# Moving the SSD scan's per-head factors, exponentials and norm weights to ScalarE, spreading the sampled queries over sequences, and moving a v chunk into the scan

## The chip, the cores and the metric

The kernel runs on one core of one Trainium2 chip. The metric is the device time of one execution in microseconds (us), lower is better. The core has five engines, each with its own queue that runs in order: TensorE (PE in the profile), VectorE (DVE), ScalarE (ACT), GpSimd (POOL) and SyncE (SP), which here issues the DMAs. What one engine needs of another it waits for by semaphores.

## The reference

One layer of a decoder for a prompt of 1024 new tokens and for 8 sequences of 8 new tokens each (the sampled tokens, with states carried over). Token mixing has two parallel parts, an HGRN2 recurrence with 8 heads and a Mamba-2 SSD scan with 16 heads in 2 groups. The change lies in the scan, cut here to its core:

```python
def ssd_scan(xs, dt, a, bm, cm, s0):
    # h_t = exp(dt_t a) h_{t-1} + dt_t x_t B_t^T, y_t = h_t C_t (per head), in chunks of 128
    cum = jnp.cumsum(log_a, axis=2)
    seg = cum[:, :, :, None] - cum[:, :, None, :]
    decay = jnp.exp(jnp.where(causal, seg, -jnp.inf))
    cb = jnp.einsum('cbtgn,cbsgn->cbtsg', cm, bm)
    y_intra = jnp.einsum('cbtsg,cbtsgr,cbsgrp->cbtgrp', cb, decay, xdt)
    to_end, from_start = jnp.exp(cum[:, :, -1:] - cum), jnp.exp(cum)
    # from chunk to chunk, with the state s:
    y = jnp.einsum('btgn,bgrpn->btgrp', c_c, s) * fs_c[..., None]
    s = cd_c[..., None, None] * s + jnp.einsum('bsgn,bsgr,bsgrp->bgrpn', b_c, te_c, xdt_c)
# then: y = (y + d_skip * xs) * silu(z); y = rmsnorm(y, in 2 groups of 512) * m_norm
```

The sampled sequences go through the same scan, each from its own state `state_ssm`, and their new states are outputs. Behind the mixing come the output projection, a squared-ReLU MLP and norms.

## The kernel before

All products that need it are split into a high and a low fp32r part and summed from three matmuls (lines L203 to L205 of the profile). The program's stages follow each other: normalising and a first chunk of v, the scan stage (function `ssd`), the 8 HGRN heads (`hgrn_head`), the output projection, and the MLP.

In `ssd`, `conv_tile` computes one tile of 128 features of x, B and C (a GEMM, the convolution and its activation) and puts it into DRAM. `ssd_group(gi)` then scans one group of 8 heads over 8 chunks of 128 tokens, reading back from there. Per chunk:

- `ssd_pre` starts the loads: `em` (for each of 8 heads a 128x128 field of cumulative sums, L671), `x` (L673), `sz` (L675);
- `ssd_mid` makes `xdt` and `te` (`ssd_x`), and in `decay` turns `em` into the masked decay matrix: subtract the head's own sum and clip at 0 (L682, eight times), exponential (L684), product (L685);
- `ssd_prod` has the matmuls `pyi` (state times C, L699), `pdd` (the chunk's share of the new state, L701) and `py` (inside the chunk, L712), with the factor `fs` on `pyi` (L714);
- `ssd_end` calls `ssd_out`: gate (L748), square sum (L750), scaling (L752), transposes `pyt` on PE (L755), norm weights `ms` (L757), store.

After chunk 3 `ssd_sample` does the sampled tokens of the group. Its loop over j (four pairs of heads) loads eight states `s0` (L800; `ss` in the profile), transposes them (`pst`, L804), splits them, multiplies by the sampled C (`pis`, L808 and L809), takes each sequence's own part by predicated copies (`own_sequence`, L240), scales the states on GpSimd (L811), adds the new share (`pds` L245 and L246, L816) and stores them (L818).

Between the steps, `fill(n)` emits n tiles of other GEMMs from a list of generators (`filler`): chunks of z and of v (`z_chunk`, `v_chunk`, 9 token tiles each: 8 of 128 tokens, one of the 64 sampled). Their products lie in DRAM until later; head h of HGRN reads back its part of v (`vt`, `vs`). The order of instructions on each engine is set by a scheduler that simulates the program; what stands in a queue on the chip is then fixed. Tiles come from pools: a tag has a number of buffers (`bufs`), and a new tile of a tag waits until the oldest use has been given up. The tag `em` has 4, shared by the chunks' `em`, the sampled tokens' `ems` and `bmh`, and the states `s0`. The tags of `c2` have 2 or 3.

Of the kernel before, what the change touches and what calls it, by code (L numbers as in the profile page):

```python
# [6 lines left out]
F32 = mybir.dt.float32  # L7
F32R = mybir.dt.float32r
# [7 lines left out]
P = 128  # L16
# [3 lines left out]
NB = 8  # L20
# [37 lines left out]
class Kernel:  # L58
# [472 lines left out]
    def ssd(self):  # L531
        nc, a = self.nc, self.a
        with ExitStack() as es:
            g = self.g = es.enter_context(self.tc.tile_pool(name="sd", bufs=2, reuse_waits="tile"))
            self.dsk = g.tile([P, MH], F32, name="dsk", bufs=1)
            nc.sync.dma_start(self.dsk, a["d_skip"][0].partition_broadcast(P))
            self.cs = g.tile([P, 12, 27], F32, name="cs", bufs=1)
            self.filler = []
            for f in (10, 8, 0, 1, 2, 3):
                self.conv_tile(f)  # L540
            for j in range(2):
                for _ in self.z_chunk(j):
                    pass
            self.filler = [self.z_chunk(2), self.z_chunk(3)]
            self.ssd_group(0)
            self.fill(18)
            for f in (11, 9, 4, 5, 6, 7):
                self.conv_tile(f)
            self.filler = [self.v_chunk(1), self.v_chunk(2)]
            for q in range(3):  # L550
                pt = self.ps.tile([P, 512], F32, name=self.nm("pcs"), tag="tp", bufs=2)
                for j in range(4):
                    nc.tensor.transpose(pt[0:27, j * P:(j + 1) * P], self.cs[:, 4 * q + j, :], self.ident)
                crow = self.c2("ms", [P, 512])
                nc.scalar.copy(crow[0:27, :], pt[0:27, :])
                cols = slice(q * 512, (q + 1) * 512)
                nc.sync.dma_start(a["o_cvp"][0, 0, :, cols], crow[0:3, :])
                nc.sync.dma_start(a["o_cvs"][0, :, :, cols].rearrange("b j c -> (b j) c"), crow[3:27, :])
                self.fill(1)
            self.ssd_group(1)  # L560
            self.fill(18)
            self.filler = [self.v_chunk(3)]

# [114 lines left out]
    def decay(self, em, cbm, rows, c, h0):  # L678

        nc = self.nc  # L680
        for h in range(8):
            nc.vector.tensor_scalar(out=em[:, h, :], in0=em[:, h, :], scalar1=self.cum[0:rows, c, h0 + h:h0 + h + 1],  # L682
                                    scalar2=0.0, op0=ALU.subtract, op1=ALU.min)
        nc.scalar.activation(em, em, AF.Exp)  # L684
        nc.vector.tensor_tensor(out=em, in0=em, in1=bc(cbm, 1, 8), op=ALU.mult)  # L685
# [6 lines left out]
    def ssd_prod(self, gi, c, st):  # L692
# [20 lines left out]
        if c > 0:  # L713
            nc.vector.tensor_tensor(out=te, in0=pi.rearrange("p (h d) -> p h d", d=HD),  # L714
                                    in1=bc(self.fs[:, c, h0:h0 + 8], 2, HD), op=ALU.mult)
        nc.vector.tensor_tensor(out=x, in0=py, in1=x, op=ALU.add)
# [8 lines left out]
    def ssd_final(self, gi, st):  # L725
# [6 lines left out]
        nc.sync.dma_start(a["o_smp"][0, 0, 8 * gi:8 * gi + 8].rearrange("(j h) p n -> (h p) j n", h=2), so)  # L732

    def ssd_x(self, x, rows, c, h0):

        nc = self.nc
        xdt, te = self.c2("xdt", [P, 8, HD]), self.c2("te", [P, 8, HD])
        r = slice(0, rows)
        nc.vector.tensor_tensor(out=xdt[r], in0=x[r], in1=bc(self.dtt[r, c, h0:h0 + 8], 2, HD), op=ALU.mult)
        nc.vector.tensor_tensor(out=te[r], in0=xdt[r], in1=bc(self.te[r, c, h0:h0 + 8], 2, HD), op=ALU.mult)  # L740
        nc.vector.tensor_tensor(out=x[r], in0=x[r], in1=bc(self.dsk[r, h0:h0 + 8], 2, HD), op=ALU.mult)
        return xdt, te

    def ssd_out(self, gi, y, sz, rows, col):
# [9 lines left out]
        for j in range(4):  # L754
            nc.tensor.transpose(pt[:, j, 0:rows], y[r_, j * P:(j + 1) * P], self.ident[0:rows, 0:rows])  # L755
        ms = self.c2("ms", [P, 4, P])
        nc.vector.tensor_tensor(out=ms[:, :, 0:rows], in0=pt[:, :, 0:rows], in1=bc(self.mn[:, 4 * gi:4 * gi + 4], 2, rows),  # L757
                                op=ALU.mult)
        for c, s_ in self.places(col // P):
            nc.sync.dma_start(self.mixd[KO + 4 * gi:KO + 4 * gi + 4, :, c].rearrange("k p t -> p k t"), ms[:, :, s_])  # L760

    def ssd_sample(self, gi):
# [30 lines left out]
        ted = self.stacked(g, te.rearrange("p h d -> p (h d)"), 512, "ted")  # L793
        cts = self.beside(g, bt[:, 1, :], "cts", "bts")
        yf = self.c2("ms", [P, 4, P])
        nc.gpsimd.memset(yf, 0.0)
        for j in range(4):
# [3 lines left out]
            for hf in range(2):  # L801
# [4 lines left out]
                self.split(sth, stl, pt)  # L806
                pi = ps.tile([P, 4, P], F32, name=self.nm("pis"), tag="sm", bufs=3)
                nc.tensor.matmul(pi, cts, sth, start=True, stop=False)  # L808
                nc.tensor.matmul(pi, cts, stl, start=False, stop=True)  # L809
                self.own_sequence(yf[:, j, :], pi, 4 * hf)  # L810
            nc.gpsimd.tensor_tensor(out=s0, in0=s0, in1=bc(self.cds[:, hh // 2, :], 2, P), op=ALU.mult)  # L811
# [67 lines left out]
    def hgrn_head(self, h):  # L879
# [22 lines left out]
        nc.scalar.activation(LF, A, AF.Ln, bias=self.lb[:, h:h + 1], scale=self.oml[:, h:h + 1])  # L902
        self.fill(4)
        K = A
# [45 lines left out]

        self.fill(9)

# [635 lines left out]
```

## Time and profile before

| what | us |
|---|---|
| median of 3 runs (lowest, highest) | 1901.96 (1899.98, 1903.06) |
| the profiled execution, its span | 1905.25, 1903.5 |
| PE busy | 1816.3 (95%) |
| VectorE busy | 1345.6 (71%) |
| ScalarE busy | 865.6 (45%) |
| GpSimd busy | 447.6 (24%) |

An engine's busy time is the sum over its instructions; the share is of the span. The rows further down come from the one profiled execution, and the positions in them are microseconds from its start: group 0 of the scan runs from about 160 to 358, with convolution tiles beside it, group 1 from about 409 to 535, and head 0 of HGRN behind it.

### The profile page before, as it was taken

The numbers are of one execution on the slowest core, as the hardware profiler recorded it, in microseconds if no ns is written. First come the engines' busy times: TensorE is split into PE (matmuls) and PEld (weight loads), VectorE is DVE, ScalarE is ACT, GpSimd is POOL, SyncE is SP. The second block draws the span as 40 slices with busy tenths as digits, with TensorE's granted clock in tenths as the row PEclk, the third lists the DMA queues.
The fourth block names the chain that finished last, engine by engine and source line by source line (L and its number), as shares of the span: only waits on it lengthen the run. The fifth ranks groups of instructions, "written<-read, shape, count | busy, mean of one in ns | idle before, by whom it ended". The sixth has DMA issues, their size and how long they took to land.

```text
span 1903.5 us, 35681 instructions
## 1 busy us (share of the span) xinstructions
PE 1816.3 (95%) x13352; PEld 1742.5 (92%) x13352; DVE 1345.6 (71%) x2769; ACT 865.6 (45%) x1891; POOL 447.6 (24%) x540
## 2 busy tenths in 40 slices
PE   7989999799589999999989998999999999999998
PEld 7989988699389999999989998999999999999998
DVE  7676779777755766776684357778887757777762
ACT  8566445552234444444442355455455553323322
POOL 5110011001111333332210036223322322322320
PEclk9999999799789999999999999999999999999999
DMA  8434455445441222222167674366555586755622
GB/s 264 125 101 128 126 164 156 124 124 151 133 116 48 81 71 81 82 82 68 51 198 227 178 217 125 105 207 212 184 176 194 199 286 226 249 165 186 226 83 78
DMA packets 329495, 285.47 MB, mean 150 GB/s; under 512 B 26197, under 2 KB 268481, under 8 KB 329322
## 3 DMA queue, kind: packets, MB, share of 16 engines
q1 hardware_dynamic: 329322, 283.19, 47.6%
q8 instruction: 105, 1.72, 0.4%
q14 instruction: 68, 0.56, 0.1%
HBM read 184.61 MB, written 98.24 MB: 149 GB/s over the span
## 4 chain that ended last, share of the span: by engine, by line
PE 78%; DVE 8%; DMA 6%; ACT 4%; issue 3%; POOL 1%; SPq 1%; DVEq 0%; ACTq 0%; POOLq 0%
PE sx L1318 15%; PE mm L205 11%; PE mm L203 11%; PE mm L204 11%; PE sy L1318 7%; PE sz L1318 4%; DVE wl L199 1%; PE py L712 1%; PE mk L203 1%; PE mk L204 1%; PE mk L205 1%; DVE acc L601 1%; DVE em L682 1%; PE pf L203 1%; PE pf L205 1%
## 5 line engine op out<-in xcount | busy, mean ns | idle before, releaser
L198 ACT CAST wh<-wr 128x512 fp32r<-128x512 f32 (+3 forms) x354 | 202.4, 582 | 266.9 <-PE mm L204 90.1
L199 DVE TENSOR_TENSOR wl<-wr,wh 128x512 fp32r<-128x512 f32 (+3 forms) x354 | 233.0, 664 | 107.3 <-ACT wh L198 99.9
L203 PE MATMUL mm<-hh,wh 128*128 128x384 f32 (+1 forms) x840 | 280.0, 333 | 10.3 <-ACT raw L587 10.3
L204 PE MATMUL mm<-hl,wh 128*128 128x384 f32 (+1 forms) x840 | 281.2, 335 | 0.0
L205 PE MATMUL mm<-hh,wl 128*128 128x384 f32 (+1 forms) x840 | 280.8, 334 | 0.0
L1318 PE MATMUL sx<-th,wh 128*128 128x272 f32 x1248 | 243.7, 291 | 7.2 <-ACT u L1371 2.9
L1318 PEld LDWEIGHTS sx<-th,wh 128*128 128x128 f32 x1248 | 196.4, 189 | 12.1 <-ACT u L1371 6.0
L1318 PE MATMUL sx<-th,wl 128*128 128x272 f32 x624 | 180.3, 289 | 0.0
L203 PEld LDWEIGHTS mm<-hh,wh 128*128 128x128 f32 x840 | 159.5, 190 | 13.5 <-ACT raw L587 12.3
L205 PEld LDWEIGHTS mm<-hh,wl 128*128 128x128 f32 x840 | 159.2, 190 | 5.4 <-issue 4.4
L204 PEld LDWEIGHTS mm<-hl,wh 128*128 128x128 f32 x840 | 159.5, 190 | 2.2 <-issue 1.2
L203 PE MATMUL mm<-wh,hh 128*128 128x260 f32 (+1 forms) x512 | 149.2, 292 | 3.3 <-ACT st L373 2.2
L205 PE MATMUL mm<-wh,hl 128*128 128x260 f32 (+1 forms) x512 | 147.6, 289 | 0.1
L204 PE MATMUL mm<-wl,hh 128*128 128x260 f32 (+1 forms) x512 | 146.7, 287 | 0.0
L1318 PE MATMUL sy<-th,wh 128*128 128x272 f32 x736 | 143.1, 290 | 2.6 <-ACT th L198 2.6
L1275 POOL TENSOR_TENSOR ws<-wr 128x512 f32<-128x512 f32 (+2 forms) x36 | 45.2, 1256 | 424.8 <-DMA wr<-in_w_down_dram 195.9
L1318 PE MATMUL sx<-td,wh 128*128 128x272 f32 x672 | 131.7, 289 | 1.7 <-ACT acc L1463 1.3
L1318 PEld LDWEIGHTS sy<-th,wh 128*128 128x128 f32 x736 | 116.4, 189 | 3.8 <-ACT th L198 2.8
L1318 PEld LDWEIGHTS sx<-th,wl 128*128 128x128 f32 x624 | 118.1, 190 | 0.1
L203 PE MATMUL mm<-mh,wh 128*128 128x272 f32 x384 | 111.8, 293 | 4.4 <-DVE res L1169 4.4
L204 PE MATMUL mm<-ml,wh 128*128 128x272 f32 x384 | 111.6, 291 | 0.0
L205 PE MATMUL mm<-mh,wl 128*128 128x272 f32 x384 | 111.2, 290 | 0.0
(507 smaller groups left out, 4832.6 us busy)
## 6 DMA issues: line engine op xcount, KB each, us to landing
td<-th SPq DMA_DIRECT2D x112, 272.0 KB, 2.9
td<-td SPq DMA_DIRECT2D x112, 272.0 KB, 5.3
wr<-in_w_in_dram SPq DMA_DIRECT2D x44, 512.0 KB, 4.7
wr<-in_w_out_dram SPq DMA_DIRECT2D x32, 512.0 KB, 4.6
wr<-in_w_up_dram SPq DMA_DIRECT2D x32, 512.0 KB, 4.1
u2d<-u SPq DMA_DIRECT2D x50, 272.0 KB, 2.1
ur<-u2d SPq DMA_DIRECT2D x50, 272.0 KB, 4.9
wr<-in_w_down_dram SPq DMA_DIRECT2D x64, 192.0 KB, 2.7
```

Source lines behind the costliest of these rows:

```text
L198: nc.scalar.copy(hi, x)
L199: (engine or nc.vector).tensor_tensor(out=lo, in0=x, in1=hi.bitcast(F32), op=ALU.subtract)
L203: nc.tensor.matmul(ps, sh, mh, start=start, stop=False)
L204: nc.tensor.matmul(ps, sh, ml, start=False, stop=False)
L205: return nc.tensor.matmul(ps, sl, mh, start=False, stop=stop)
L601: nc.vector.scalar_tensor_tensor(out=acc[:, 0:w], in0=raw[:, j:j + w], scalar=self.cw[:, j, f:f + 1], in1=acc[:, 0:w], op0=ALU.mult, op1=A ...
L682: nc.vector.tensor_scalar(out=em[:, h, :], in0=em[:, h, :], scalar1=self.cum[0:rows, c, h0 + h:h0 + h + 1], scalar2=0.0, op0=ALU.subtract, ...
L712: nc.tensor.matmul(py[:, h, :], em[:, h, :], xdt[:, h, :], start=True, stop=True)
L1275: self.nc.gpsimd.tensor_tensor(out=out_, in0=x, in1=y, op=op)
L1318: nc.tensor.matmul(acc, w_[:, k, :], b_[:, cols], start=first and k == 0 and q == 0, stop=k == nk - 1 and q == 2, skip_group_check=True)
```

## The change

- `decay`: one minimum over the whole tile on VectorE, min(em, cum), and eight exponentials on ScalarE, one for each head, with the negated sum (`ncum`, new) as bias, instead of eight subtractions with clipping and one exponential.
- The factors by head, `te` in `ssd_x` and `fs` on `pyi`, become eight ScalarE copies of 64 columns with a per-partition factor each (`per_head`), and the norm weights four copies of 128 columns, instead of one VectorE product each.
- The sampled queries: GpSimd spreads C over a tile `cm` (for each sequence a 128-wide stationary matrix that is zero outside that sequence's columns), so that 16 matmuls of 128 columns per j add up in one PSUM tile; a ScalarE copy takes it out. The predicated copies go. `cm` is a tile of the tag `em`, whose buffers stay 4.
- Fillers: group 0 gets z2, z3 and v1, group 1 v2 and v3; head 0 of HGRN has none.

```diff
...
             self.dsk = g.tile([P, MH], F32, name="dsk", bufs=1)
             nc.sync.dma_start(self.dsk, a["d_skip"][0].partition_broadcast(P))
             self.cs = g.tile([P, 12, 27], F32, name="cs", bufs=1)
+            self.ncum = g.tile([P, NT, MH], F32, name="ncum", bufs=1)
+            nc.scalar.activation(self.ncum[:, 0:NC, :], self.cum[:, 0:NC, :], AF.Copy, scale=-1.0)
+            nc.scalar.activation(self.ncum[0:NS, NC, :], self.cum[0:NS, NC, :], AF.Copy, scale=-1.0)
             self.filler = []
             for f in (10, 8, 0, 1, 2, 3):
                 self.conv_tile(f)
             for j in range(2):
                 for _ in self.z_chunk(j):
                     pass
-            self.filler = [self.z_chunk(2), self.z_chunk(3)]
+            self.filler = [self.z_chunk(2), self.z_chunk(3), self.v_chunk(1)]
             self.ssd_group(0)
-            self.fill(18)
+            self.fill(27)
             for f in (11, 9, 4, 5, 6, 7):
                 self.conv_tile(f)
-            self.filler = [self.v_chunk(1), self.v_chunk(2)]
+            self.filler = [self.v_chunk(2), self.v_chunk(3)]
             for q in range(3):
                 pt = self.ps.tile([P, 512], F32, name=self.nm("pcs"), tag="tp", bufs=2)
                 for j in range(4):
...
                 self.fill(1)
             self.ssd_group(1)
             self.fill(18)
-            self.filler = [self.v_chunk(3)]
 
     C2 = {"sz": 3, "x": 3, "xdt": 3, "te": 2, "st": 3, "ms": 2}
 
...
     def decay(self, em, cbm, rows, c, h0):
 
         nc = self.nc
+        nc.vector.tensor_tensor(out=em, in0=em, in1=bc(self.cum[0:rows, c, h0:h0 + 8], 2, em.shape[2]), op=ALU.min)
         for h in range(8):
-            nc.vector.tensor_scalar(out=em[:, h, :], in0=em[:, h, :], scalar1=self.cum[0:rows, c, h0 + h:h0 + h + 1],
-                                    scalar2=0.0, op0=ALU.subtract, op1=ALU.min)
-        nc.scalar.activation(em, em, AF.Exp)
+            nc.scalar.activation(em[:, h, :], em[:, h, :], AF.Exp, bias=self.ncum[0:rows, c, h0 + h:h0 + h + 1])
         nc.vector.tensor_tensor(out=em, in0=em, in1=bc(cbm, 1, 8), op=ALU.mult)
 
     def ssd_mid(self, gi, c):
...
         for h in range(8):
             nc.tensor.matmul(py[:, h, :], em[:, h, :], xdt[:, h, :], start=True, stop=True)
         if c > 0:
-            nc.vector.tensor_tensor(out=te, in0=pi.rearrange("p (h d) -> p h d", d=HD),
-                                    in1=bc(self.fs[:, c, h0:h0 + 8], 2, HD), op=ALU.mult)
+            self.per_head(te, pi.rearrange("p (h d) -> p h d", d=HD), self.fs[:, c, h0:h0 + 8])
         nc.vector.tensor_tensor(out=x, in0=py, in1=x, op=ALU.add)
         if c > 0:
             nc.vector.tensor_tensor(out=x, in0=x, in1=te, op=ALU.add)
...
         nc.scalar.copy(so, pt)
         nc.sync.dma_start(a["o_smp"][0, 0, 8 * gi:8 * gi + 8].rearrange("(j h) p n -> (h p) j n", h=2), so)
 
+    def per_head(self, out, x, f):
+
+        for h in range(8):
+            self.nc.scalar.activation(out[:, h, :], x[:, h, :], AF.Copy, scale=f[:, h:h + 1])
+
     def ssd_x(self, x, rows, c, h0):
 
         nc = self.nc
         xdt, te = self.c2("xdt", [P, 8, HD]), self.c2("te", [P, 8, HD])
         r = slice(0, rows)
         nc.vector.tensor_tensor(out=xdt[r], in0=x[r], in1=bc(self.dtt[r, c, h0:h0 + 8], 2, HD), op=ALU.mult)
-        nc.vector.tensor_tensor(out=te[r], in0=xdt[r], in1=bc(self.te[r, c, h0:h0 + 8], 2, HD), op=ALU.mult)
+        self.per_head(te[r], xdt[r], self.te[r, c, h0:h0 + 8])
         nc.vector.tensor_tensor(out=x[r], in0=x[r], in1=bc(self.dsk[r, h0:h0 + 8], 2, HD), op=ALU.mult)
         return xdt, te
 
...
         for j in range(4):
             nc.tensor.transpose(pt[:, j, 0:rows], y[r_, j * P:(j + 1) * P], self.ident[0:rows, 0:rows])
         ms = self.c2("ms", [P, 4, P])
-        nc.vector.tensor_tensor(out=ms[:, :, 0:rows], in0=pt[:, :, 0:rows], in1=bc(self.mn[:, 4 * gi:4 * gi + 4], 2, rows),
-                                op=ALU.mult)
+        for j in range(4):
+            nc.scalar.activation(ms[:, j, 0:rows], pt[:, j, 0:rows], AF.Copy, scale=self.mn[:, 4 * gi + j:4 * gi + j + 1])
         for c, s_ in self.places(col // P):
             nc.sync.dma_start(self.mixd[KO + 4 * gi:KO + 4 * gi + 4, :, c].rearrange("k p t -> p k t"), ms[:, :, s_])
 
...
         nc.sync.dma_start(te[NS:P], te[R])
         ted = self.stacked(g, te.rearrange("p h d -> p (h d)"), 512, "ted")
         cts = self.beside(g, bt[:, 1, :], "cts", "bts")
+        cm = g.tile([P, NB, 2, NB, TS], F32R, name=self.nm("cm"), tag="em", bufs=4)
+        nc.gpsimd.memset(cm.bitcast(F32), 0.0)
+        for b in range(NB):
+            nc.gpsimd.tensor_copy(cm[:, b, :, b, :], cts.bitcast(F32).rearrange("p (a b t) -> p a b t", a=2, t=TS)[:, :, b, :])
         yf = self.c2("ms", [P, 4, P])
-        nc.gpsimd.memset(yf, 0.0)
         for j in range(4):
             hh = h0 + 2 * j
             s0 = self.em("ss0", [P, NB, P])
...
                     nc.tensor.transpose(pt[:, q, :], s0[:, 4 * hf + q, :], self.ident)
                 sth, stl = (g.tile([P, 4, P], F32R, name=self.nm("stb"), tag=t, bufs=2) for t in ("ct", "btok"))
                 self.split(sth, stl, pt)
-                pi = ps.tile([P, 4, P], F32, name=self.nm("pis"), tag="sm", bufs=3)
-                nc.tensor.matmul(pi, cts, sth, start=True, stop=False)
-                nc.tensor.matmul(pi, cts, stl, start=False, stop=True)
-                self.own_sequence(yf[:, j, :], pi, 4 * hf)
+                if hf == 0:
+                    pi = ps.tile([P, P], F32, name=self.nm("pis"), tag="sm", bufs=3)
+                for q in range(4):
+                    b = 4 * hf + q
+                    for i, st_ in enumerate((sth, stl)):
+                        nc.tensor.matmul(pi, cm[:, b].rearrange("p a s t -> p (a s t)"), st_[:, q, :],
+                                         start=b == 0 and i == 0, stop=b == NB - 1 and i == 1)
+            nc.scalar.copy(yf[:, j, :], pi)
             nc.gpsimd.tensor_tensor(out=s0, in0=s0, in1=bc(self.cds[:, hh // 2, :], 2, P), op=ALU.mult)
             for hf in range(2):
                 pd = ps.tile([P, 4, P], F32, name=self.nm("pds"), tag="sm", bufs=3)
...
         self.sigmoid_from_exp(A)
         LF = wk("lf")
         nc.scalar.activation(LF, A, AF.Ln, bias=self.lb[:, h:h + 1], scale=self.oml[:, h:h + 1])
-        self.fill(4)
         K = A
         nc.vector.tensor_scalar(out=K, in0=A, scalar1=self.noml[:, h:h + 1], scalar2=self.oml[:, h:h + 1],
                                 op0=ALU.mult, op1=ALU.add)
...
         nc.vector.tensor_tensor(out=K128, in0=KEB[:, 0:SEQ].rearrange("p (c b t) -> p c b t", b=4, t=32)[:, :, 0:2],
                                 in1=bc(fac[:, :, 9:11], 3, 32), op=ALU.mult)
 
-        self.fill(9)
 
         Dm = wk("dm")
         nc.vector.tensor_tensor(out=Dm[:, 0:SEQ].rearrange("p (b t) -> p b t", t=32),
```

SyncE issues the DMAs; these are its rows around the sampled states of group 1, before. `ss` is a state tile (its first number tells the tiles apart), L800 its load, L818 its store, and `em` the loads for chunks 5 to 7:

```order
L800 DMA ss_889_5634<-in_state_ssm_dram 128x8x128
...
L800 DMA ss_902_5706<-in_state_ssm_dram 128x8x128
...
L818 DMA o_sms_dram<-ss_889_5634 128x8x128
...
L800 DMA ss_915_5778<-in_state_ssm_dram 128x8x128
...
L818 DMA o_sms_dram<-ss_902_5706 128x8x128
L800 DMA ss_928_5850<-in_state_ssm_dram 128x8x128
...
L818 DMA o_sms_dram<-ss_915_5778 128x8x128
L671 DMA em_5950<-cumd 128x1024
L671 DMA em_6063<-cumd 128x1024
L818 DMA o_sms_dram<-ss_928_5850 128x8x128
L671 DMA em_6125<-cumd 128x1024
```

After the change, the same place (the load is now L808, the store L830, the `em` load L673):

```order
L808 DMA ss_916_6149<-in_state_ssm_dram 128x8x128
...
L830 DMA o_sms_dram<-ss_916_6149 128x8x128
...
L808 DMA ss_928_6225<-in_state_ssm_dram 128x8x128
...
L830 DMA o_sms_dram<-ss_928_6225 128x8x128
L808 DMA ss_940_6301<-in_state_ssm_dram 128x8x128
L830 DMA o_sms_dram<-ss_940_6301 128x8x128
L808 DMA ss_952_6377<-in_state_ssm_dram 128x8x128
L673 DMA em_6484<-cumd 128x1024
L830 DMA o_sms_dram<-ss_952_6377 128x8x128
L673 DMA em_6614<-cumd 128x1024
L673 DMA em_6693<-cumd 128x1024
```

A load stood ahead of the store before it; now each load stands behind it, and takes the buffer that the store gives up.

PE's rows around j=2 and j=3 of group 1's loop before. `mm` with `hh` and `wl` is a GEMM tile (here the last filler work is the 320-column block of head 0's f), `pst` the transposes of a state, `pis` and `pds` the sampled products, and `pyi` the first matmul of the scan behind the sample:

```order
L804 MATMUL pst_5796<-ident,ss_915_5778 128x128 x4
L205 MATMUL mm_6328<-hh_94,wl_6299 128x384
...
L205 MATMUL mm_6354<-hh_97,wl_6299 128x320
L808 MATMUL pis_5805<-stb_5801,cts_5629 128x512
...
L804 MATMUL pst_5852<-ident,ss_928_5850 128x128 x4
...
L804 MATMUL pst_5868<-ident,ss_928_5850 128x128 x4
...
L246 MATMUL pds_5889<-bml_5559,ted_5626 128x512
L699 MATMUL pyi_5984<-st_5468,ct_5398 128x512
```

After; the first rows here are j=1 (`ss_928`), the next ones j=2 (`ss_940`) and j=3 (`ss_952`):

```order
L812 MATMUL pst_6245<-ident,ss_928_6225 128x128 x4
L204 MATMUL mm_6952<-hl_102,wh_6896 128x320
...
L205 MATMUL mm_6952<-hh_97,wl_6897 128x320
L820 MATMUL pis_6236<-stb_6232,cm_6138 128x128
...
L812 MATMUL pst_6303<-ident,ss_940_6301 128x128 x4
L812 MATMUL pst_6321<-ident,ss_940_6301 128x128 x4
...
L812 MATMUL pst_6379<-ident,ss_952_6377 128x128 x4
L812 MATMUL pst_6397<-ident,ss_952_6377 128x128 x4
...
L700 MATMUL pyi_6518<-st_5950,ct_5880 128x512
```

The f GEMM used to end ahead of the transposes of j=3, and now it ends right behind those of j=1; j=2 and j=3 come with no other work.

PE behind group 1's last transposes, before:

```order
L729 MATMUL pst_6228<-ident,st_6191 128x128 x4
L755 MATMUL pyt_6250<-ident,x_6127 128x128 x4
L203 MATMUL mm_6405<-wh_6387,hh_90 128x260
L204 MATMUL mm_6405<-wl_6388,hh_90 128x260
L205 MATMUL mm_6405<-wh_6387,hl_98 128x260
```

And after:

```order
L729 MATMUL pst_6823<-ident,st_6776 128x128 x4
L760 MATMUL pyt_6845<-ident,x_6695 128x128 x4
L203 MATMUL mm_7025<-hh_90,wh_7017 128x384
L204 MATMUL mm_7025<-hl_98,wh_7017 128x384
L205 MATMUL mm_7025<-hh_90,wl_7018 128x384
```

Before, nine v tiles of 260 columns (the first three matmuls of 24 in the first are shown) stand ahead of head 0's Q GEMM; now the Q GEMM, with 384 columns, follows at once.

## Rows read from the trace of the kernel before

**Rows 1.** The page's first part: busy us, share, instructions of each engine.

```profile
PE 1816.3 (95%) x13352; PEld 1742.5 (92%) x13352; DVE 1345.6 (71%) x2769; ACT 865.6 (45%) x1891; POOL 447.6 (24%) x540
```

**Rows 2.** Windows: busy us and instruction counts of each engine in four stretches.

```profile
core 0: us, PE busy (x) PEld busy (x) DVE busy (x) ACT busy (x) POOL busy (x), PEclk, DMA share, GB/s
240.00:340.00 100.00, 97.30 (x611) 87.36 (x611) 84.20 (x214) 51.16 (x113) 14.48 (x23) 1.00 0.52 153
340.00:380.00 40.00, 28.06 (x150) 25.32 (x149) 29.61 (x74) 21.70 (x52) 3.25 (x8) 0.74 0.44 127
480.00:535.00 55.00, 31.08 (x133) 20.87 (x132) 45.84 (x121) 15.61 (x38) 6.40 (x16) 0.70 0.37 109
535.00:577.00 42.00, 39.81 (x283) 39.20 (x282) 17.24 (x20) 16.03 (x29) 8.48 (x13) 0.94 0.49 138
```

**Rows 3.** PE timeline, end of group 0: start, us, line, idle before and its releaser.

```profile
354.65 1.11 PE L755 MATMUL pyt<-ident,x 128*128 128x128 f32 x4 [6.74 <-ACT x L752]
```

**Rows 4.** PE timeline, end of group 1, from the last filler to the last transpose.

```profile
480.15 0.31 PE L205 MATMUL mm<-hh,wl 128*128 128x320 f32 x1
480.30 0.39 PE L808 MATMUL pis<-stb,cts 128*128 128x512 f32 x1
480.52 0.40 PE L245 MATMUL pds<-bmh,ted 128*128 128x512 f32 x1
...
481.84 0.63 PE L804 MATMUL pst<-ident,ss 128*128 128x128 f32 x4 [0.50 <-DMA ss<-in_state_ssm_dram]
...
506.77 2.56 PE L755 MATMUL pyt<-ident,x 64*128 64x64 f32 x12 [14.09 <-ACT x L752]
...
513.83 2.08 PE L701 MATMUL pdd<-te,btok 128*128 128x512 f32 x2 [4.50 <-DVE te L740]
...
534.46 1.09 PE L755 MATMUL pyt<-ident,x 128*128 128x128 f32 x4 [0.19 <-DVE ms L757]
```

**Rows 5.** Groups by line and shape, VectorE, the scan stage: busy us, mean ns.

```profile
L682 DVE TENSOR_SCALAR em<-em,cum 128x128 f32<-128x128 f32 x128 | 29.4, 300 | 6.2 <-DMA em<-cumd 5.2 <-issue 1.0
...
L685 DVE TENSOR_TENSOR em<-em,cbm 128x1024 f32<-128x1024 f32 x16 | 19.2, 1215 | 0.3 <-ACT em L684 0.3
...
L240 DVE COPY_PREDICATED ms<-seqm,pis 128x128 f32<-128x128 uint32 x64 | 18.7, 298 | 6.7 <-PE pis L809 5.8
...
L740 DVE TENSOR_TENSOR te<-xdt,te 128x512 f32<-128x512 f32 x16 | 10.9, 682 | 0.0
```

**Rows 6.** Groups by line and shape, ScalarE, the scan stage.

```profile
L592 ACT COPY raw<-mm 128x64 f32<-128x64 f32 x12 | 2.7, 226 | 0.0
...
L684 ACT ACTIVATE em<-em 128x1024 f32<-128x1024 f32 x16 | 16.9, 1057 | 30.9 <-DVE em L682 30.9
...
L750 ACT ACTIVATE sz<-x 128x512 f32<-128x512 f32 x16 | 10.0, 625 | 26.4 <-DVE x L748 26.4
...
L752 ACT ACTIVATE x<-x,yr128y 128x512 f32<-128x512 f32 x16 | 11.3, 716 | 8.8 <-DVE yr128y L164 8.0 <-PE pyt L755 0.9
```

**Rows 7.** ScalarE timeline, head 0 of the HGRN stage.

```profile
543.82 0.30 ACT L198 CAST vsh<-vs 128x128 fp32r<-128x128 f32 x1 [4.50 <-DMA vs<-vd]
...
557.68 0.38 ACT L373 COPY st<-mm 128x260 f32<-128x260 f32 x1 [2.51 <-PE mm L205]
560.57 0.38 ACT L373 COPY st<-mm 128x260 f32<-128x260 f32 x1 [2.51 <-PE mm L205]
```

**Rows 8.** PE timeline, head 0 of the HGRN stage.

```profile
577.10 0.60 PE L981 MATMUL pke<-ident,ke 128*128 128x128 f32 x4
```

**Rows 9.** SyncE timeline, end of group 1: DMA issues.

```profile
477.78 0.37 SPq L800 DMA_DIRECT2D ss<-in_state_ssm_dram  x1
...
488.87 0.39 SPq L818 DMA_DIRECT2D o_sms_dram<-ss  x1
```

**Rows 10.** The sampled states' stores (L818): issue to landing.

```profile
DMA to landing us min/median/max: 3.2/3.2/3.2
```

## The prediction

> **What bounds the kernel now.** I read the page first. TensorE (PE) is busy 1816.3 us of a span of 1903.5 [rows 1], so time is lost or won where PE idles, or where PE work is added to a full stretch. The busy times by stretch come next [rows 2]. In group 0 of the scan PE is nearly full (97.30 of 100 us from 240 to 340). From 340 to 380, where group 0 ends, it is busy 28.06 of 40; from 480 to 535, where group 1 ends, 31.08 of 55, with VectorE (DVE) at 45.84 and ScalarE (ACT) at 15.61. Head 0 of the HGRN stage, right behind, is full again (39.81 of 42). PE idles 12 us in the one end and 24 in the other.
>
> The PE timeline says who is late there. At the end of group 0 the transpose `pyt` (L755) waits 6.74 us in one piece for the ScalarE copy L752 [rows 3]. At the end of group 1 the last filler matmul (head 0's f GEMM) starts at 480.15; behind it PE has only the sampled tokens and chunks 4 to 7, waits 14.09 us for L752 at 506.77 and 4.50 us for `te` at 513.83, and reaches the last `pyt` at 534.46 [rows 4]. That is 54.3 us with no filler. L752 itself waits for VectorE there (15.61 busy against 45.84): VectorE is the late one in the tails.
>
> **The ScalarE moves.** VectorE loses, per chunk, the eight L682 (2.40 us of busy time), and three 128x512 products like L740 (.68 each: `te`, `pyi` times `fs`, `ms`); it gains one 128x1024 minimum, which I price at L685's 1.215 [rows 5]. The L682 records overlap, so the real gain is between 2.05 and 3.2; I take 2.5, 40 us over 16 chunks. The sample loses 64 predicated copies of .298 [rows 5], 18.7 us.
>
> ScalarE gains, per chunk, 8+8 copies of 128x64, 8 exponentials of 128x128 less one of 1.057, and 4 copies of 128x128. A 128x64 copy takes .226; a per-partition factor costs .716 against .625 at 128x512, so .09 more [rows 6]; hence .226 to .317 for a piece, and by the line through .226 and .625, .28 to .37 for 128x128. With the middles: 16x.27 + 12x.325 - 1.06 = 7.2 us a chunk, some 115 in all. Group 0 has room: ScalarE is busy 51.16 of 100 between 240 and 340 [rows 2], and about 4 chunks' work is added there, 29. It then stands at .8, not full. PE covers it while filler is queued; what crowds into the chain of a full stretch I put at +1 (-3 to +8).
>
> The Trainium skill, "ScalarE: Activation LUTs", section Rules for kernel authors, says to use VectorE and not ScalarE for a multiplication. Row for row the trace agrees (.68 for a 128x512 product on VectorE, about 2.2 for the eight pieces on ScalarE). By that rule the moves lose about 1.5 us for each product wherever ScalarE is the one waited for; that is the third rival below.
>
> **The moved v tiles.** One v tile takes PE 2.89 us (its copies start at 557.68 and 560.57) [rows 7]; nine take 26.0. They leave head 0 and enter group 0. In head 0 PE spends 42.6 us from the last `pyt` (534.46) to `pke` (577.10) [rows 4, 8]. Without the nine tiles 16.6 remain, if the chain to `ke` on ScalarE and VectorE is ready by then. Today that chain stands 4.50 us for the load of `vs` [rows 7], which the earlier v3 removes. I take 17.5 left, 25 saved; if the chain stays as long as it is, about 21 left and 21 saved. In group 0 the tiles cost 26.0 where PE is full. Net +1 (0 to +5). What they can fill is the stall at group 0's end, where order puts six filler blocks now and two before. Those 12 idle us, with VectorE relieved there as well, I price at -10 (0 to -12).
>
> **The sampled tokens.** The new tile `cm` is taken from the tag `em`, which has 4 buffers. During the sample one holds chunk 4's `em` (read by `py` behind the sample), one `bmh`, one `cm`: a single one is left for the state tile `s0`. The order on SP shows it: load, store, load, store, where before a load ran ahead of the store. Each j of the loop then needs the former store to land. The trace has every piece for j=3 of group 1: load issued at 477.78, store at 488.87, so 11.1; landing of a store 3.2 [rows 9, 10]; 14.3 us per j. Before, the last filler started at 480.15 and the last store at 488.87, 8.7 later. Now the last filler stands just behind j=1's transposes. From a j's transposes to its store takes 7.0 (481.84 to 488.87 [rows 4, 9]); about 5 of them are left when the filler ends. So: 5.0 + 3.2 + 11.1 + 3.2 + 11.1 = 33.6 from the end of the filler to the last store, 24.9 more than before. Behind the stores in SP's queue stand the `em` loads of chunks 6 and 7 (that of 5 stands just ahead of the last store), and the `x` and `sz` loads; `decay`, `xdt`, `te` and `pdd` wait for those.
>
> Off this go: one j's matmuls that no longer lie in the full stretch before the filler's end, some 3 us; and VectorE's relief. In the tail that is 3 chunks x 2.5 + 2 j's x 8 x .298 = 12.3; against it ScalarE's pieces stand in the same chains (`te` 2.2 for .68, exponentials 2.6 for 1.06), so I credit half, 6. That gives 24.9 - 3 - 6 = +16 (6 to 25: a loop with its waits hidden, none hidden).
>
> In group 0 the same loop stands beside filler: between the transposes of one j and the next, order has some 105 PE rows, at about .12 each 13 us, against 14.3 needed: 1 per j where no more is late, +2 (0 to 8).
>
> **The new products.** Per j there are 16 matmuls of 128 columns instead of 4 of 512. A matmul of 512 columns starts .22 after the one ahead of it (480.30 to 480.52) [rows 4]; a tile of 24 matmuls of 260 columns takes 2.89, .12 each [rows 7]. The trace has no fp32r matmul of 128 columns: by columns alone .055, by the 512-column row at most .22. I take .09, between .055 and the 260-column row's .12. Five of the eight j's lie under full PE: 80x.09 - 20x.22 = +3 (0 to +13).
>
> The Trainium skill, "TensorE: Matmul & The Clock Gate", section Back-to-back issue gap, gives about 81 ns for a sustained matmul of 128 columns with its weight load and 131 ns for 512. Ours of 512 takes 220, so the trace differs for the long one. By the page's pair the term would be 80x.081 - 20x.131 = +3.9, an estimate.
>
> **Sum.** Moved tiles +1, stall of group 0 -10, sample in group 1 +16, in group 0 +2, products +3, ScalarE +1: +13. Against the profiled execution's own 1905.25 this is 1918.3; the median of the runs, 1901.96, is 3.3 lower than that, so 1915. GpSimd's clearing of `cm` and its eight small casts (two samples) cost nothing here: they stand before the loop, where `ted` and the first load are awaited; uncovered they would be a few us per group.
>
> **The rivals.** *VectorE's relief decides* (.30). The tails are bound by VectorE (45.84 of 55 [rows 2]); if the relief counts in full at both ends and the load-store chain runs beside the sample's other work, the tail of group 1 shortens by 12 instead of growing, and the stall of group 0 goes whole. Then +1 - 12 - 12 + 0 + 0 = -23: 1882 to 1895, 1890 with the smaller terms. It decides when chunk 4's `em` is set free early, so that a second `s0` buffer exists. For it: 59 us less VectorE work. Against it: SP's order.
>
> *No measurable change* (.10). The loop costs some 10 per j beside idle PE, about half of the +16; with the stall filled the sum is about 0: 1898 to 1906. 0.2% is about what a measurement of this kernel can tell from no change, 3.8 us.
>
> *ScalarE becomes the bound* (.10). If its in-order queue is what the chunks wait for, each chunk's chain grows by 1.5 for `te` and some .5 for the exponentials, 2 us on 16 chunks, +32 instead of what is credited to VectorE (6) : about +13 + 26, 1941. Against it: .8 busy in group 0, and 15.61 of 55 in the tail, where some 25 are added.
>
> *My forecast, slower by the single s0 buffer* (.50); its own range is 1906 to 1926.
>
> The range reaches from the first rival's middle to between forecast and the third: 1888 to 1936. Faster .30, within .10, slower .60 (the forecast and the third).
>
> **What the new profile would show.** Right: s0 loads each issued only after a store has landed, 13 to 15 us apart in group 1; last filler to last `pyt` about 70 us instead of 54.3; from there to `pke` 17 to 21; no wait over 3 us at group 0's end, and group 0 longer by about 20. Products: 16 `pis` in about 1.5 us. Wrong: a tail of under 50 us, or two s0 loads in flight; ScalarE over 90% busy in group 0 with PE waiting on it would point to the third rival; PE idle before `pke` would mean the chain to `ke` was what head 0 needed its tiles for.

## The result and the profile after

The changed kernel takes 1922.27 us (median of 4 runs, 1919.42 to 1924.78) against 1901.87 for the kernel before (4 runs; 1901.96 was the median of the first 3): a ratio of 1.0108 (95% interval 1.009 to 1.0125), 20.4 us slower. The forecast was 1915, slower, range 1888 to 1936. The span of the profiled execution grew from 1903.5 to 1920.9, by 17.4.

First the engines over the whole span, from the page of the changed kernel:

```profile
PE 1830.6 (95%) x13448; PEld 1755.6 (91%) x13448; DVE 1298.8 (68%) x2529; ACT 962.9 (50%) x2355; POOL 459.4 (24%) x556
```

Against [rows 1], VectorE has 46.8 us less to do and ScalarE 97.3 more, and the kernel is slower all the same. The windows of the changed kernel say where:

```profile
core 0: us, PE busy (x) PEld busy (x) DVE busy (x) ACT busy (x) POOL busy (x), PEclk, DMA share, GB/s
340.00:380.00 40.00, 36.32 (x217) 34.24 (x216) 30.14 (x64) 33.04 (x103) 2.75 (x11) 0.96 0.51 153
480.00:535.00 55.00, 41.17 (x191) 32.43 (x189) 17.08 (x26) 10.66 (x30) 5.69 (x3) 0.72 0.45 135
535.00:577.00 42.00, 21.25 (x86) 14.75 (x86) 25.36 (x59) 31.12 (x118) 7.20 (x15) 0.61 0.25 73
```

Read beside [rows 2]: the hole at 340 to 380 is closed (36.32 busy for 28.06, granted clock .96 for .74). Between 480 and 535 VectorE and ScalarE have almost nothing to do (17.08 and 10.66 of 55): PE's long waits there are for a transfer (next rows). The scan's last phase has moved behind 535, where head 0 used to run at full PE.

The PE timeline of that tail (start, us, instruction, idle before and its releaser):

```profile
493.67 0.31 PE L205 MATMUL mm<-hh,wl 128*128 128x320 f32 x1
493.81 0.23 PE L820 MATMUL pis<-stb,cm 128*128 128x128 f32 x1
...
505.87 1.94 PE L812 MATMUL pst<-ident,ss 128*128 128x128 f32 x8 [7.06 <-DMA ss<-in_state_ssm_dram]
...
518.66 1.94 PE L812 MATMUL pst<-ident,ss 128*128 128x128 f32 x8 [3.22 <-DMA ss<-in_state_ssm_dram]
...
532.05 1.08 PE L700 MATMUL pyi<-st,ct 128*128 128x512 f32 x2
546.20 1.70 PE L760 MATMUL pyt<-ident,x 64*128 64x64 f32 x8 [13.07 <-ACT x L757]
...
552.48 2.08 PE L702 MATMUL pdd<-te,btok 128*128 128x512 f32 x2 [3.23 <-ACT te L737]
...
574.55 1.12 PE L760 MATMUL pyt<-ident,x 128*128 128x128 f32 x4 [0.98 <-ACT x L757]
...
595.93 1.09 PE L991 MATMUL pke<-ident,ke 128*128 128x128 f32 x4
```

and SyncE's issues in it (L808 loads a state tile, L830 stores it, L673 loads a chunk's `em`):

```profile
486.41 0.38 SPq L808 DMA_DIRECT2D ss<-in_state_ssm_dram  x1
496.80 0.38 SPq L830 DMA_DIRECT2D o_sms_dram<-ss  x1
501.85 0.37 SPq L808 DMA_DIRECT2D ss<-in_state_ssm_dram  x1
511.62 0.38 SPq L830 DMA_DIRECT2D o_sms_dram<-ss  x1
514.88 0.37 SPq L808 DMA_DIRECT2D ss<-in_state_ssm_dram  x1
522.91 0.34 SPq L673 DMA_DIRECT2D em<-cumd  x1
524.40 0.38 SPq L830 DMA_DIRECT2D o_sms_dram<-ss  x1
530.44 0.81 SPq L673 DMA_DIRECT2D em<-cumd  x2
```

The loads are 15.4 and 13.0 us apart, each behind a store, as forecast (14.3). The wait of `pst` for the load, .50 us before [rows 4], is now 7.06 and 3.22. From the last filler matmul to the last `pyt` it takes 80.9 us (493.67 to 574.55) where it took 54.3 [rows 4]; from there to `pke` 21.4, where it took 42.6 [rows 4, 8].

ScalarE's new pieces in the groups by line (busy us, mean ns of one; records that overlap count once in the busy time):

```profile
L685 ACT ACTIVATE em<-em,ncum 128x128 f32<-128x128 f32 x128 | 40.0, 398 | 15.3 <-DVE em L683 12.8 <-issue 2.5
...
L737 ACT ACTIVATE te<-xdt,te 128x64 f32<-128x64 f32 x128 | 33.3, 351 | 9.2 <-DVE xdt L744 6.7 <-DVE x L718 2.5
```

### The profile page after: what moved, and what is told of

Same layout as the page of the kernel before. It is cut to its first block, busy times and chain, and to the rows that moved or that the text cites. A ratio compares the mean times of both kernels' runs of the same rounds, so it can differ in the third digit from the quotient of the medians.

```text
span 1920.9 us, 36110 instructions
## 1 busy us (share of the span) xinstructions
PE 1830.6 (95%) x13448; PEld 1755.6 (91%) x13448; DVE 1298.8 (68%) x2529; ACT 962.9 (50%) x2355; POOL 459.4 (24%) x556
## 4 chain that ended last, share of the span: by engine, by line
PE 79%; DMA 7%; DVE 6%; ACT 4%; issue 2%; POOL 1%; SPq 0%; DVEq 0%; ACTq 0%; POOLq 0%
PE sx L1328 16%; PE mm L205 11%; PE mm L203 11%; PE mm L204 11%; PE sy L1328 7%; PE sz L1328 4%; DVE wl L199 1%; PE py L713 1%; DMA ur<-u2d 1%; PE mk L204 1%; PE mk L203 1%; PE mk L205 1%; DMA em<-cumd 1%; PE pf L203 1%; PE pf L205 1%
```

## The experiments

Theory A: the change loses its time by the one state tile in flight, because `cm` takes a buffer of `em`; fillers and ScalarE moves are worth about what they look like. Theory B: the ScalarE moves lengthen the chains of the tails. A third question was what the moved fillers are worth by themselves. Ratios are to runs of the kernel before that were made beside each kernel; for the experiments the medians of those were 1902.82 to 1904.91, so a ratio is not the quotient of two medians of this table. The last column has positions in the profiled execution.

| kernel | median us | ratio (95%) | last filler, last `pyt`, `pke` of head 0 |
|---|---|---|---|
| before | 1901.96 | | 480.15, 534.46, 577.10 |
| the change | 1922.27 | 1.0108 (1.009 to 1.0125) | 493.67, 574.55, 595.93 |
| change, `cm` in its own buffer | 1895.54 | 0.9951 (0.993 to 0.9972) | 498.06, 545.45, 567.21 |
| change, only `tok` smaller | 1925.70 | 1.0105 (1.0089 to 1.0121) | 493.71, 575.12, 596.25 |
| fillers alone | 1888.45 | 0.9913 (0.9893 to 0.9933) | 485.33, 539.54, 561.30 |
| ScalarE moves alone | 1905.32 | 1.0007 (0.999 to 1.0024) | 480.11, 533.88, 576.95 |
| fillers and ScalarE moves | 1892.64 | 0.9928 (0.9901 to 0.9954) | 491.24, 545.73, 570.01 |
| sample alone, `cm` in `em` | 1939.45 | 1.0171 (1.0145 to 1.0196) | 492.25, 569.74, 611.46 |
| sample alone, own buffer | 1908.58 | 1.0016 (1.0 to 1.0031) | 485.84, 535.21, 577.30 |

**`cm` in a buffer of its own.** To make room, `tok` of the conv tiles gives up a buffer.

```diff
-        cm = g.tile([P, NB, 2, NB, TS], F32R, name=self.nm("cm"), tag="em", bufs=4)
+        cm = g.tile([P, NB, 2, NB, TS], F32R, name=self.nm("cm"), tag="cm", bufs=1)
...
-            tok = g.tile([P, 3, P], F32, name=self.nm("tok"), tag="tok", bufs=3)
+            tok = g.tile([P, 3, P], F32, name=self.nm("tok"), tag="tok", bufs=2)
```

> The changed kernel with the tile cm in a buffer of its own, so that two state tiles are in flight again as before (the conv tiles' tok gets 2 buffers instead of 3 to make room). Theory A, the single s0 buffer is what the tail of group 1 lost: loads run ahead of stores again, filler's end to last pyt falls from 81 us to 50-58, and the time to 1895-1902 (ratio to before 0.996-1.000). Theory B, the ScalarE moves lengthen the chains of the tail: it stays at 75-81 and the time at 1915-1922 (1.007-1.011).

It takes 1895.54, 26.7 under the change. Its SyncE timeline, with loads ahead of stores again:

```profile
461.92 0.38 SPq L808 DMA_DIRECT2D ss<-in_state_ssm_dram  x1
469.01 0.39 SPq L830 DMA_DIRECT2D o_sms_dram<-ss  x1
472.24 0.38 SPq L808 DMA_DIRECT2D ss<-in_state_ssm_dram  x1
475.22 0.39 SPq L830 DMA_DIRECT2D o_sms_dram<-ss  x1
478.89 0.37 SPq L808 DMA_DIRECT2D ss<-in_state_ssm_dram  x1
487.31 0.39 SPq L830 DMA_DIRECT2D o_sms_dram<-ss  x1
...
500.42 0.39 SPq L830 DMA_DIRECT2D o_sms_dram<-ss  x1
```

The tail from last filler to last `pyt` falls from 80.9 to 47.4, and the last `pyt` comes 29.1 earlier (the filler is spread differently, so the sum is the safer number). This is theory A; theory B would have left the time where it was. It is still 7.1 us above the fillers alone (1888.45, further down; the two kernels' runs do not overlap): ScalarE moves and sample together cost something even with two state tiles in flight.

**The control for `tok`.** Only the second pair of lines of that diff, in the changed kernel.

> Control: the changed kernel with tok at 2 buffers instead of 3 and nothing else, which the kernel with cm in a buffer of its own had too. If the third tok buffer does nothing: 1919-1926, the changed kernel's time. If it matters: above 1926, and the buffer of cm is then worth more than e1 shows.

It takes 1925.70, with an interval that is the change's own. So it was the buffer of `cm`, not the third `tok`.

**The kernel before, with an unused tile held.** A tile of the tag `em` is taken ahead of the loop and read into only behind it.

```diff
+        dm = self.em("dum", [P, NB, P])
+        nc.gpsimd.memset(dm[:, 0, 0:2], 0.0)
         yf = self.c2("ms", [P, 4, P])
...
+        nc.gpsimd.tensor_copy(dm[:, 0, 0:1], yf[:, 3, 0:1])
         yv = yf.rearrange("p j (h d) -> p (j h) d", d=HD)
```

> The kernel before, with an unused tile of the tag em held through the sample's loop, so that one state tile is in flight, as after the change; nothing else differs. Theory A: the tail of group 1 grows by 20-27 us, group 0 by 0-8, time 1920-1930 (1.010-1.015). Theory B: the load-store chain hides beside the other work, within 0.3% of before (1.000-1.003).

It takes 1959.76, ratio 1.0292 (1.0262 to 1.0322): 57 us, twice what theory A gave, and above its range. PE's waits in this kernel (us in total, times, longest), from 200 to 640:

```profile
PE pyt L755 <- ACT x L752: 38.8, 6, 13.5
PE pst L806 <- DMA ss<-in_state_ssm_dram: 20.9, 3, 8.3
```

The wait for the load is there, and group 0 suffers too. Its loads are 20 to 24 us apart:

```profile
242.63 0.37 SPq L802 DMA_DIRECT2D ss<-in_state_ssm_dram  x1
259.49 0.39 SPq L820 DMA_DIRECT2D o_sms_dram<-ss  x1
262.80 0.38 SPq L802 DMA_DIRECT2D ss<-in_state_ssm_dram  x1
282.82 0.39 SPq L820 DMA_DIRECT2D o_sms_dram<-ss  x1
286.47 0.37 SPq L802 DMA_DIRECT2D ss<-in_state_ssm_dram  x1
```

In the changed kernel they are 13.9 to 15.5 apart there (236.83, 252.32, 266.20, 280.51), with PE busy 99.89 of 100 us between 240 and 340. With the predicated copies in VectorE's queue a state tile is held 17 to 20 us from load to store, and with one buffer all of that stands in the loop.

**The sample's part alone**, with `cm` in `em` and in its own buffer: the diff of the change for `ssd_sample`, and the same with the two lines above.

> The kernel before with only the sample's part of the change (cm in the tag em, 16 products of 128 columns per j, no predicated copies), so one state tile in flight. If the held buffer is the whole cost and the fillers do not matter, as much as the unused tile cost: 1950-1962 (1.025-1.032). If the 18.7 us of predicated copies that VectorE loses shorten each j, less: 1925-1945 (1.012-1.023). If the changed kernel's 27 us in group 1 are all there is: 1922-1932.

> The kernel before with the sample's part of the change, cm in a buffer of its own (tok 2 instead of 3): two state tiles in flight. If PE pays for the narrow products where it is full (128 of .12 against 32 of .22 us, +8) and VectorE's 18.7 us are not waited for: 1906-1912 (1.002-1.005). If VectorE's relief decides in the two tails: 1890-1898 (0.994-0.998).

They take 1939.45 and 1908.58, so the buffer costs 30.9, against 57 with the predicated copies. The products without them do shorten each j: with one buffer a state tile of group 0 is held 11.3 to 15.3 us here, against 16.9 to 20.0. With two tiles in flight the part costs 0.16%, at the edge of what can be told (the interval begins at 1.0). In the profile the last filler ends 5.7 later, the tail gives 4.9 back, and `pke` comes .2 later than before; that the 5.7 are the narrow products on a full PE, and the 4.9 VectorE's relief, was not separated. VectorE's busy time falls by 12.8 us, and what that brings is at most those 4.9.

**The ScalarE moves alone**: `decay`, `per_head` and the norm weights of the change, with fillers and sample as before.

> The kernel before with only the ScalarE moves (min and eight exponentials, te, fs, norm weights), sample and fillers as before. Theory A: PE hides them in the full stretches and VectorE's relief takes some of the two stalls, 1890-1903 (0.994-1.001). Theory B: each chain of the tails grows by 1.5 to 3 us per chunk, 1910-1920 (1.004-1.010).

The ratio is 1.0007. This is the clearest run of the study. Its window of the tail, in the columns of the windows above:

```profile
480.00:535.00 55.00, 32.27 (x129) 20.54 (x127) 36.33 (x83) 36.63 (x134) 10.23 (x16) 0.71 0.36 107
```

VectorE is busy 36.33 instead of 45.84 and ScalarE 36.63 instead of 15.61 [rows 2], and the tail takes 53.8 us instead of 54.3. Theory B is out, and of theory A the ratio fits but not the reason: no stall became shorter. VectorE's waits between 480 and 535 show where about half of its 9.5 us went (us in total, times, longest; before, then here):

```profile
DVE xdt L739 <- DMA x<-xtd: 1.2, 1, 1.2
DVE xdt L745 <- DMA x<-xtd: 6.0, 3, 3.9
```

VectorE now waits for the loads of `x`, 6.0 us instead of 1.2. They are issued only when `pyt` has read an earlier `x`: SyncE waits 2.8 us for `pyt` there (2.4 before). That is a second round trip by DMA in the tail, set by the 3 buffers of `x`; more of them were not tried. How much of ScalarE's 21 us lies in the chain as well was not worked out.

**The fillers alone.**

> The kernel before with only the fillers moved (v1 into group 0, v3 out of head 0). Theory A, as the changed kernel's trace has it: group 0 ends 14 us later (26 of tiles, 12 of stall gone), head 0 saves 21, so 1893-1897 (0.995-0.998). Rival C, without VectorE's relief the stall at group 0's end stays although PE has filler (VectorE is the late one): group 0 ends 20-26 later, and the time is 1900-1907 (0.999-1.003).

It takes 1888.45, ratio 0.9913, better than both expectations, and is the fastest kernel of the study. Its window at group 0's end:

```profile
340.00:380.00 40.00, 38.19 (x242) 37.41 (x241) 30.40 (x68) 29.35 (x70) 7.03 (x19) 1.00 0.53 150
```

PE is busy 38.19 of 40 at a granted clock of 1.00, where it had 28.06 at .74 [rows 2]. The nine tiles cost 26.0 us and the last filler ends only 5.2 later: the move gave back 21, more than the 12 that PE idled, and the low clock went with the hole. If the work of 28.06 us at .74 would take 20.8 at 1.00 (an estimate from these two rows), the clock is worth 7 of the other 9. The rival put on record for this run, that VectorE keeps the hole open, is wrong. The tail is as before (54.2), and head 0 saves 20.9 (21.8 left from the last `pyt` to `pke`).

**Fillers and ScalarE moves, and fillers with the unused tile**: the change with `ssd_sample` as before; and the fillers' kernel with the lines of the unused tile.

> The changed kernel with the sample as before: fillers and ScalarE moves together. If the two add up (fillers alone 0.9913, ScalarE moves alone 1.0007): 1886-1893 (0.991-0.995). If VectorE's relief shortens the tails once PE is filled at group 0's end: 1875-1885. If ScalarE crowds the fuller group 0: 1893-1903.

> Fillers moved, and the unused tile of the tag em held through the sample's loop: the fillers' kernel (1888.5) plus one state tile in flight. If the nine tiles in group 0 hide the loop's waits there, as in the changed kernel, only the tail of group 1 grows: 1915-1928 (1.007-1.013). If they do not, the 57 us of the same tile without the move come back: 1938-1948 (1.018-1.024).

The first takes 1892.64: within the intervals the parts add up, and VectorE's relief is not seen here either. It is 4.2 above the fillers alone; in the profiles its last filler ends 5.9 later, and its tail is as long (54.5). The second takes 1946.78, ratio 1.0213 (1.0178 to 1.0247), 58 above the fillers alone; its last `pyt` of group 0 comes at 389.85, against 352.52. What the held buffer costs in group 0 can be read from PE's busy time between 160 and 400 in each pair of kernels:

| one buffer less in | PE busy with two tiles in flight, with one | lost |
|---|---|---|
| the kernel before (unused tile) | 224.62, 208.61 | 16.0 |
| the fillers alone (unused tile) | 238.19, 222.19 | 16.0 |
| the sample alone (`cm`) | 229.38, 219.83 | 9.6 |
| the change (`cm`) | 236.60, 233.73 | 2.9 |

The nine tiles alone hide nothing (16.0 in both), and the shorter j alone leaves 9.6. Only in the whole change is the loop of group 0 almost hidden; which parts of it that takes was not separated further.

**Work held back for the tail.** In the kernels so far the filler ends before the tail, with head 0's f GEMM pulled ahead. Here a one-column copy on GpSimd into the weight tile makes the loads wait: v3 for j=1's state tile of group 1, the f GEMM for the state after chunk 5.

```diff
+        if gate is not None:
+            nc.gpsimd.tensor_copy(raw[:, 0, 0:1], gate)
...
+            if gi == 1 and j == 1:
+                self.filler.append(self.v_chunk(3, gate=s0[:, 0, 0:1]))
...
+            if gi == 1 and c == 5:
+                self.wf0 = self.weight(self.a["w_in"][0, :, C_F:C_F + P], KO, P, gate=st[:, 0:1])
```

> Fillers moved (e2), and the last v chunk and head 0's f GEMM held back: the loads of their weights wait for the second state tile of group 1's sample and for the state after chunk 5, so that PE has this work (26 and 12 us) in the tail. If the tail is idle PE that any work fills: the tail's idle 22 us are used and the time is 1868-1880 (0.982-0.988). If what stands before the tail is bound by VectorE (62 of 80 us busy there), the stall only moves forward: 1883-1895 (0.990-0.996).

> The same two things held back in the kernel with fillers and ScalarE moves and the sample as before (e4, 1892.6). If VectorE's 40 us count once PE has work in the tail: 1865-1876, below the fillers' kernel held back. If not: 1873-1890, as far above it as e4 is above e2 (some 4 us).

> The same two things held back in the changed kernel with cm in a buffer of its own (e1), in which VectorE has some 59 us less to do. If VectorE is what bounds group 1 once PE has work in the tail, the relief counts here for the first time: 1862-1878 (0.978-0.987), below the fillers' kernel held back in the same way. If ScalarE takes the place of VectorE in the chains, as in the ScalarE moves alone: 1875-1890.

They take 1905.46 (1.0005, 0.9994 to 1.0016), 1902.95 (0.999, 0.9981 to 0.9999) and 1912.08 (1.004, 1.0026 to 1.0054): 17, 10 and 17 above the same kernels without it, and above every range on record for them. The window before the tail in the fillers' kernel, then in the first of the three:

```profile
400.00:480.00 80.00, 80.00 (x601) 73.72 (x600) 62.20 (x126) 24.08 (x57) 6.43 (x4) 1.00 0.52 151
400.00:480.00 80.00, 62.88 (x387) 52.37 (x387) 57.36 (x119) 18.72 (x43) 6.53 (x6) 0.79 0.42 119
```

PE was busy 80.00 of 80 there and is now busy 62.88. The hole moved ahead, with its low clock (.79 for 1.00). No engine is full in it: VectorE 57.36, ScalarE 18.72. A reading that fits is that group 1 is bound by the length of its chains once PE has no other work, and that the filler only chooses where PE idles. It is not shown: the chains were not shortened in any run, and neither a gate at another place nor the cost of the gate itself was tried.

## Why the prediction was right, and by how much its terms were off

The direction, the cause and the place were right: one state tile in flight, loads behind stores, group 1's tail. Without it the same change is faster than before (0.9951). That the size came so near is in part luck: in the profile the forecast of +13 is 4.4 off, while its steps are off by -5.5, -2.9, +10.5, +3.9 and -1.4 and partly cancel. By the steps, measured between the two profiles:

- *Up to the filler's end in group 1*, forecast +19 (tiles 26, stall -10, group 0's sample 2, products 3, ScalarE 1, and 3 off): 493.67 - 480.15 = 13.5. The stall was undersized. The fillers alone show 21 instead of 10: the term counted idle time at most, and not the matmuls that ran at the low clock. That granted clock (.74) stood in [rows 2] and was not priced. Group 0 ends 14.1 later (its last `pyt` at 371.49 for 357.38), where about 20 was forecast, and no wait of PE at its end is over 1.2. Its sample, forecast 2, cost 2.9 by PE's busy time (table above). By kernels the 13.5 are 5.2 with the fillers alone, 5.9 more with the ScalarE moves (forecast 1, at most 8) and 2.4 more with the sample.
- *The narrow products*, forecast .09 each: seven that end in a row take .89 in the changed kernel, of which the last is .22 long, so (.89 - .22)/6 = .11 us each. In the forecast's own sum that is 80 x .11 - 20 x .22 = +4.4 instead of +3. A nearer row stood in the trace before: the four 128-column f32 matmuls of `pke` take .60 in a row [rows 8], .27 each by their records, so (.60 - .27)/3 = .11.

```profile
484.68 0.22 PE L820 MATMUL pis<-stb,cm 128*128 128x128 f32 x1
486.19 0.89 PE L820 MATMUL pis<-stb,cm 128*128 128x128 f32 x7
```

- *From the filler's end to the last store*, forecast 33.6: 524.40 - 493.67 = 30.7. Close, by durations that all stood in the trace: from load to store it takes 9.8 and 9.5 instead of 11.1, and one load follows its store by 5.1 instead of 3.2.
- *VectorE's relief in the tail*, credited with 6: this term failed. From last store to last `pyt` it took 45.6 and now takes 50.2, longer by 4.5, so the credit was off by 10.5. Two things are in it. The relief is worth next to nothing: the ScalarE moves alone shorten a tail of 54 by .5. And `cm` holds a second wait that the forecast did not have: the loads of `em` for chunks 6 and 7 come at 530.44, 6.0 after the last store, where the last of them came 2.9 after it before. The load before the change:

```profile
491.80 0.32 SPq L671 DMA_DIRECT2D em<-cumd  x1
```

  After it, SyncE waits for the last `pis`, which reads `cm` (us in total, times, longest, between 440 and 560):

```profile
SPq L673 <- PE pis L820: 5.6, 1, 5.6
```

  With `cm` in its own buffer the same stretch takes 45.0 (500.42 to 545.45), with every ScalarE piece in it. So the 4.5 go with the buffer, though eight pieces of `te` take 2.02 us in a row on ScalarE, where VectorE took .68 [rows 5]:

```profile
550.40 2.02 ACT L737 ACTIVATE te<-xdt,te 128x64 f32<-128x64 f32 x8 [1.31 <-DVE xdt L744]
```

- *Head 0*, forecast 17.5 left: 21.4; the bound of 21 was the better value. The forecast let the earlier v3 remove the wait for `vs` (4.50 [rows 7]); 2.68 of it are still there, since the load of `vs` stands behind the last `mixd` store in SyncE's queue, as before:

```profile
583.20 0.30 ACT L198 CAST vsh<-vs 128x128 fp32r<-128x128 f32 x1 [2.68 <-DMA vs<-vd]
```

- The rest of the program is 1.4 shorter; over the kernels of the table it takes 1324 to 1332, so this says nothing. Sum: 13.5 + 26.6 - 21.3 - 1.4 = 17.4, with 26.6 for the whole tail (80.9 for 54.3; the forecast had about 70).

Of the rivals, VectorE's relief did not decide anywhere; VectorE's busy time fell by 46.8, not 59. ScalarE as the bound did not come either: busy 74.05 of 100 between 140 and 240 with PE at 99.71. That rival was also added up wrongly: 32 in place of a credit of 6 is 38 more, not 26, so it stood for about 1953 and not 1941. The rule of the Trainium skill, "ScalarE: Activation LUTs", section Rules for kernel authors, to use VectorE for a multiplication, agrees with the pieces (2.02 for .68); in the sum of the ScalarE moves alone nothing of it can be told (1.0007). The Trainium skill, "TensorE: Matmul & The Clock Gate", section Back-to-back issue gap, gives 81 ns for 128 columns; measured here were about 110.

## What to carry to other kernels

Ask of a new tile whose buffers it takes, and read the order of loads and stores on the DMA queue: one buffer fewer turned loads that ran ahead into a chain of landing, work and landing. Its price was 27, 31 or 57 us, most where the tile was held longest. Later users of the same buffers pay too, as chunks 6 and 7 did with `em`. Busy time taken off an engine gained nothing here where that engine then waited for a load; so look at what it will wait for next before moving work. A hole on PE was worth more than its idle time (21 us for 12), with the granted clock low around it; filling it was the fastest kernel here (0.9913).

## What the runs showed of the hardware that had not been expected

PE's granted clock was low in each stretch with holes that was looked at (.74 at group 0's end, .70 to .72 in the tail, .79 in the hole that the held-back work made), and with the hole at group 0's end filled it stood at 1.00; nine tiles of 26.0 us then came at 5.2.

ScalarE's short pieces have long records, .351 us on the mean for 64 columns and .398 for 128, but the records overlap. By busy time a piece is 33.3/128 = .26 and 40.0/128 = .31, near the .27 and .325 of the forecast, and eight of 64 columns in a row take 2.02, .25 each. In all ScalarE has 97.3 us more to do, where 115 was forecast.
